# Half a block of a 268 MB copy cut into seven small DMAs over 14, 2, 9, 7, 4, 12 and 16 engines

## The chip, the cores and the metric

The kernel runs on one core of one Trainium2 chip. The metric is the device time of that core in microseconds (us). The kernel does no arithmetic: all of its work is done by the core's 16 DMA engines, which copy from one HBM tensor to another. Two instruction queues issue the DMAs, that of SyncE (SP) and that of ScalarE (ACT).

## The reference

`x` is an 8192 x 8192 float32 matrix (268.44 MB), and the result is `np.fft.ifftshift(x)`. Both sides are even, so each axis is rotated by half its length: the four quadrants of 4096 x 4096 change places diagonally. Row `r` of the output is row `(r + 4096) % 8192` of the input with its left and right halves exchanged.

```python
def setup_inputs():
    return {"x": np.random.randn(8192, 8192).astype(np.float32)}

def reference(x):
    return np.fft.ifftshift(x)
```

## The kernel before

The kernel cuts the output into 64 blocks of 128 rows. One DMA moves one block, from HBM to HBM, with nothing in between: 128 rows of 32 KB, 4 MB in all. Within each row the DMA writes the left half and then the right half, and reads the input's right half and then its left one. The pattern is 128 x 2 x 4096 floats, so it comes apart into 256 contiguous pieces of 16 KB. All 16 DMA engines take part, with 16 pieces each (`rows = ENGINES * 8` gives every engine eight rows). A piece is what the trace calls a packet.

The blocks are dealt to the two queues in groups of eight: of each 1024 output rows, SP's queue takes the first four blocks and ACT's queue the last four. In program order the two queues take turns. SP therefore begins at output row 0 and ACT at row 512, and each issues 32 DMAs:

```python
for first in range(0, R, 8 * rows):
    for row in range(first, first + 4 * rows, rows):
        whole_rows(nc.sync, row)
        whole_rows(nc.scalar, row + 4 * rows)
```

No wait is written by hand. The framework puts a semaphore on every DMA and has eight of them for this kernel: in the trace SP's DMAs use four in turn and ACT's the other four. A queue issues its fifth DMA when its first has landed, its sixth when its second has, and so on. Four blocks of each queue are therefore outstanding until the end. Each of the 16 engines sees two streams of packets, SP's (queue 1 of the profile) and ACT's (queue 10), and serves both of them.

The change touches what the ACT queue issues before its second block (output row 640): the single DMA `whole_rows(nc.scalar, 512)` in the loop's first turn.

Of the kernel before, what the change touches and what calls it, by code (L numbers as in the profile page):

```python
# [1 line left out]

# [4 lines left out]


ENGINES = 16


@with_exitstack
def kernel(
    ctx: ExitStack,
    tc: tile.TileContext,
    x: bass.AP,
    out: bass.AP,
):


    nc = tc.nc
    R, C = x.shape
    hr = R // 2
    hc = C // 2
    rows = ENGINES * 8

    def whole_rows(queue, row):
        src = (row + hr) % R
        queue.dma_start(
            out=bass.AP(out.tensor, out.offset + row * C, [[C, rows], [hc, 2], [1, hc]]),  # L30
            in_=bass.AP(x.tensor, x.offset + src * C + hc, [[C, rows], [-hc, 2], [1, hc]]),
        )

    for first in range(0, R, 8 * rows):
        for row in range(first, first + 4 * rows, rows):
            whole_rows(nc.sync, row)
            whole_rows(nc.scalar, row + 4 * rows)


# [1 line left out]
_INS = ['x']  # L41
_OUTS = [((8192, 8192), 'float32')]


def kernel(**inputs):
    import numpy as _np
    import concourse.bacc as _bacc
    import concourse.tile as _tile
    from concourse import mybir as _mybir
    from concourse.bass_utils import run_bass_kernel_spmd as _run  # L50

    nc = _bacc.Bacc("TRN2", target_bir_lowering=False, num_devices=1)  # L52
    arrays, args = {}, []
    for name in _INS:
        a = _np.ascontiguousarray(inputs[name])
        if a.dtype.kind in "iu":
            a = a.astype(_np.int64)
        arrays[f"in_{name}_dram"] = a
        args.append(nc.dram_tensor(f"in_{name}_dram", a.shape, _mybir.dt.from_np(a.dtype), kind="ExternalInput").ap())
    for i, (shape, dtype) in enumerate(_OUTS):  # L60
        dt = _mybir.dt.from_np(_np.dtype(dtype))
        args.append(nc.dram_tensor(f"out_{i}_dram", shape, dt, kind="ExternalOutput").ap())
    with _tile.TileContext(nc) as tc:
        kernel(tc, *args)
    r = _run(nc, [arrays], core_ids=[0])
    got = tuple(r.results[0][f"out_{i}_dram"] for i in range(len(_OUTS)))
    return got[0]
```

## Time and profile before

| What | Value |
|---|---|
| Time, median of 3 runs | 823.04 us (822.89 to 824.0) |
| The profiled execution's own time | 823.57 us |
| Its span, first to last instruction | 821.8 us |
| DMAs | 32 from SP, 32 from ACT, 4 MB each |
| Moved | 268.44 MB read and as much written |
| A DMA from issue to landing, median | 102.2 us |
| Issue time of one DMA on its queue | 0.6 to 0.9 us for the first four, 0.56 to 0.57 us later |

The compute engines do nothing but clear a few constants (0.2 us), so the only rows to read are those of the DMA engines. The page gives their busy share and the bytes that they moved per second in 40 equal slices of 20.5 us. The trace has every single packet with its start, duration, size and queue. It doesn't name the engine of a packet, but on one engine a packet starts where the last one ended (4 ns before it, in the median), so the 16 sequences can be followed.

### The profile page before, as it was taken

Reading aid. Unit: us, or ns where it says so; the run is one execution under the profiler, and the core shown is the slowest. Engines: PE = TensorE matmul, PEld = TensorE weight load, DVE = VectorE, ACT = ScalarE, POOL = GpSimd, SP = SyncE. Lnnn points to the kernel's source line nnn. Section 1 sums busy time; section 2 is a strip of 40 time slices with the busy share of each in tenths; the row PEclk is TensorE's granted clock in tenths of the full one; section 3 lists DMA queues with packets and bytes.
Section 4 is the critical chain, followed back from the end, with each engine's and each line's share of the span. In section 5 each row is a group of like instructions: output and inputs, shape, how many; then the busy total and the mean of one; then the engine's idle time right before and its main releaser. Section 6 shows DMA issues by size and latency. Waiting matters only on the chain. (4 is left out here: it accounts for less than half of the span.)

```text
span 821.8 us, 109 instructions
## 1 busy us (share of the span) xinstructions
POOL 0.2 (0%) x4
## 2 busy tenths in 40 slices
POOL 0000000000000000000000000000000000000000
DMA  9999999999999999999999999999999999999999
GB/s 302 327 327 322 333 328 320 331 328 327 333 328 332 329 321 331 331 329 330 331 330 329 321 329 329 329 324 332 325 329 329 330 328 329 331 325 331 326 325 296
DMA packets 17408, 268.44 MB, mean 327 GB/s; under 512 B 1024, under 2 KB 1024, under 8 KB 1024
## 3 DMA queue, kind: packets, MB, share of 16 engines
q10 hardware_dynamic: 8704, 134.22, 49.8%
q1 hardware_dynamic: 8704, 134.22, 49.7%
HBM read 268.44 MB, written 268.44 MB: 653 GB/s over the span
## 5 line engine op out<-in xcount | busy, mean ns | idle before, releaser
L52 POOL MEMSET const-bfloat16-1.0<- 128x1 bf16 x1 | 0.1, 102 | 0.0
L52 POOL MEMSET const-uint8-127<- 128x1 uint8 x1 | 0.1, 102 | 0.0
L52 POOL MEMSET const-float32-0.0<- 128x1 f32 x1 | 0.1, 99 | 0.2 <-issue 0.2
L52 POOL MEMSET const-float32-1.0<- 128x1 f32 x1 | 0.1, 99 | 0.0
## 6 DMA issues: line engine op xcount, KB each, us to landing
out_dram<-in_x_dram ACTq DMA_DIRECT2D x32, 4096.0 KB, 102.2
out_dram<-in_x_dram SPq DMA_DIRECT2D x32, 4096.0 KB, 102.2
```

What stands on the lines that cost most here:

```text
L52: nc = _bacc.Bacc("TRN2", target_bir_lowering=False, num_devices=1)
```

## The change

The bytes that are copied, SP's queue and ACT's blocks from row 640 on stay as they are. Of ACT's first block (output rows 512 to 639) the right half of the first 16 rows is taken out and moved by itself, ahead of the loop. It is cut into four strips of 1024 columns (4 KB a row). Each of the first three strips is moved by two DMAs, with 14 and 2 rows, 9 and 7 rows, and 4 and 12 rows; the fourth strip is one DMA of 16 rows. A DMA of `k` rows here is a pattern of `k` x 1024 floats. The rest of the block follows in the loop as two DMAs: the left half of all 128 rows (2 MB), then the right half of the last 112 rows (1.75 MB).

The ACT queue so issues nine DMAs where it issued one.

```diff
+    def half_rows(queue, row, col, dims):
+        src = (row + hr) % R * C + (col + hc) % C
+        queue.dma_start(
+            out=bass.AP(out.tensor, out.offset + row * C + col, dims),
+            in_=bass.AP(x.tensor, x.offset + src, dims),
+        )
...
+    lead = 4 * rows
+    strip = hc // 4
+    for n, k in enumerate((14, 9, 4)):
+        col = hc + n * strip
+        half_rows(nc.scalar, lead, col, [[C, k], [1, strip]])
+        half_rows(nc.scalar, lead + k, col, [[C, ENGINES - k], [1, strip]])
+    half_rows(nc.scalar, lead, hc + 3 * strip, [[C, ENGINES], [1, strip]])
+
     for first in range(0, R, 8 * rows):
         for row in range(first, first + 4 * rows, rows):
             whole_rows(nc.sync, row)
-            whole_rows(nc.scalar, row + 4 * rows)
+            if row + 4 * rows == lead:
+                half_rows(nc.scalar, lead, 0, [[C, rows], [1, hc]])
+                half_rows(nc.scalar, lead + ENGINES, hc, [[C, rows - ENGINES], [1, hc]])
+            else:
+                whole_rows(nc.scalar, row + 4 * rows)
```

## The prediction

> **What bounds the kernel now.** I read the page first: how full the DMA engines are, and how evenly.
>
> ```profile
> span 821.8 us, 109 instructions
> DMA  9999999999999999999999999999999999999999
> GB/s 302 327 327 322 333 328 320 331 328 327 333 328 332 329 321 331 331 329 330 331 330 329 321 329 329 329 324 332 325 329 329 330 328 329 331 325 331 326 325 296
> q10 hardware_dynamic: 8704, 134.22, 49.8%
> q1 hardware_dynamic: 8704, 134.22, 49.7%
> HBM read 268.44 MB, written 268.44 MB: 653 GB/s over the span
> out_dram<-in_x_dram ACTq DMA_DIRECT2D x32, 4096.0 KB, 102.2
> out_dram<-in_x_dram SPq DMA_DIRECT2D x32, 4096.0 KB, 102.2
> ```
>
> The 16 engines are busy for 99.5% of the span, half for each queue, so nothing can be gained by filling gaps. An issue lands 102.2 us later because four blocks of each queue are outstanding, far more than an issue costs. Next I read the waits of SP's queue, to see whether the engines ever wait for an issue.
>
> ```profile
> SPq L29 <- DMA out_dram<-in_x_dram: 696.9, 28, 25.6
> ```
>
> SP waits 28 times for its own earlier DMA, with three more blocks queued behind it: the queue waits for the engines. What counts is then the rate of the engines, so I cut the span into stretches.
>
> ```profile
> 2.00:5.40 3.40, 0.00 (x0) 1.00 0.94 318
> 5.40:13.00 7.60, 0.00 (x0) 1.00 1.04 362
> 13.00:21.00 8.00, 0.00 (x0) 1.00 0.99 311
> 62.00:400.00 338.00, 0.00 (x0) 1.00 1.00 328
> 400.00:764.00 364.00, 0.00 (x0) 1.00 1.00 328
> 764.00:817.00 53.00, 0.00 (x0) 1.00 1.00 327
> 817.80:820.00 2.20, 0.00 (x0) 1.00 0.92 313
> ```
>
> The last column is GB/s, counted by packet starts, so short stretches are rough. From 62 us on it is 328, 328, 327. A packet of 16 KB takes 798 ns in the mean: 1024 packets an engine x 0.7986 = 817.8 us, which with 2.2 us before the first packet and some 1.2 us behind the last is the span. The packets say more:
> - The shortest take 608 to 611 ns (28% of them), the longest over 1100 ns (7%). An engine alone could thus do 16384 / 611 = 26.8 GB/s; at 798 ns it does 20.5, and the rest is lost to something shared.
> - From 2.2 to 5.4 us only SP's packets run; the second to fourth of each engine take 611, 645 to 690 and 611 ns. From 5.4 to 13 us both queues run and the engines are close together: 753 ns with a scatter of 34. Afterwards it is 800 ns with a scatter of 180, to the end.
> - Each engine takes a packet of SP, then one of ACT, in turns of 2 x 0.8 = 1.6 us. The engines stay together in this: at a mean instant 13.0 of 16 are in the same queue (13.3 early, 12.7 late). The 16 parts of one DMA land within 0.4 to 1.1 us, from the first to the last.
>
> **The change part by part.** The seven small DMAs give the engines unlike shares, if a DMA of k rows runs on the first k engines. No row of this trace shows a DMA with k below 16. Adding up the seven: engines 0 and 1 get 7 strips of 4 KB, 2 and 3 get 6, 4 to 6 get 5, 7 and 8 get 4, 9 to 11 get 3, 12 and 13 get 2, 14 and 15 one. In sum 64 strips, 256 KB, the bytes taken from the block. The Trainium skill, in "DMA: Bandwidth & Descriptors" (section on why a DMA increments its semaphore by 16), says that such a DMA takes the largest k up to 16 that divides its slowest dimension, on the lowest-numbered engines; no run here shows it yet.
>
> *Issuing.* ACT issues eight more DMAs ahead of row 640. Its first four issues took 667, 889, 665 and 666 ns, so 8 x 0.67 = 5.4 us, plus waits if the small DMAs use up semaphores: then ACT's left half waits for the first of them, and even SP's second block may wait for one. The cover is SP's first block: 16 packets an engine at 611 ns or more, 9.8 us of work from 2.2 us on. Before, ACT's first packet came at 5.36 us; a small DMA issued up to 5.4 us later has landed by 12 us, and SP's next block follows. Cost 0. If the cover fails, engines idle for some 3 us; if SP runs alone 5 us longer at 640 instead of 753 ns, 0.75 us is gained.
>
> *Smaller pieces.* 64 pieces of 4 KB take the place of 16 of 16 KB, three more per engine. Packets follow each other without a gap, so in proportion they cost nothing (0.15 us each, a quarter of 611); if each cost a whole packet, 3 x 0.61 = 1.8 us. Eight more DMAs write 80 more completion packets of 9 ns, 0.05 us an engine. I take 0.1 us, nearer to the gapless rows.
>
> The Trainium skill speaks against such pieces: "DMA: Bandwidth & Descriptors", Rules for kernel authors, holds that below 64 KB a transfer is mostly overhead. All seven are at most 64 KB; at the page's 2.0 us fixed cost one after the other that would be 14 us, on ACT's queue only, and the sum would stand at about 841 if nothing ran beside them. The trace has SP's packets beside them.
>
> *Unequal shares.* Engine 0 has 12 KB over the mean, engine 15 as much under it. The last engine ends 12/16 of a packet later, 0.46 to 0.6 us; the others leaving earlier help it a little. Cost 0.4 us (0 to 0.6).
>
> *The engines' phases.* While the small pieces pass, one turn is a 16 KB packet of SP and a strip, about 0.8 + 0.2 = 1.0 us. Engine 0 makes seven such turns, engine 15 one, before the regular turns of 1.6 us begin. In a cycle of 1.6 us their starts at 1, 2, ... 7 us fall on 1.0, 0.4, 1.4, 0.8, 0.2, 1.2, 0.6: evenly apart. So instead of 13 of 16 engines about 8 to 10 will be in the same queue at once. Nothing later undoes it: the engines' landings stay within 1.1 us for 820 us, so all progress equally, and an offset given at the start should stay. What that is worth no row shows directly. For a loss: counted over the packets from 14 us on, instants with 14 to 16 engines in one queue move 331.5 GB/s, those with 8 or 9 move 321.4, the mean 327.8; if all instants were like the latter, 2.0% or 16 us. In windows of 12.8 us the slope is 2.5 (+/- 1.5) GB/s per engine, which over four engines is 3%; in windows of 3.2 us it is nothing, -0.2 (+/- 1.0). For a gain: the slices of the page reach from 320 to 333; if all were like the best, 817.8 x (1 - 327/333) = 14.7 us less. Against the gain stands that the most orderly stretch, 5.4 to 13 us, is the fastest with both queues. I take a loss of 0.4%, 3.4 us: near nothing, as the long stretches are flat at 327 to 328 while the order loosens, and on the side that most readings have.
>
> Sum: 823.57 + 0 + 0.1 + 0.4 + 3.4 = 827.5 for the profiled execution, which lay 0.5 us above the median of the runs: 827 us.
>
> **The rivals.**
> *Spreading the phases helps.* Engines that start packets together, whole rows of 32 KB apart, might meet in the same part of the HBM, and not when they are quarters of a packet apart (an estimate of mine; no row shows addresses). For it: the 187 ns between 611 and 798, and the long packets. Against it: the tight start. It decides if the mean packet falls below 796 ns. At the best slice's rate 808 us, at half of it 815 us; I put it at 815. Chance 0.35. The Trainium skill has a row for this ("DMA: Bandwidth & Descriptors", Latency and other measured facts): row pitches at large powers of two slow HBM copies, 207 GB/s at 512 KiB against 214 with 4 KiB of padding. Taken as the gain here, those 3.4% would give 796 us. No run here shows it; the orderly start speaks against it.
> *No effect of the phases*, or the engines fall back into step within some turns, or the k-row DMAs don't spread as I added them up. Then only 0.5 us is left: 823.5 us. For it: 327 to 328 in every long stretch. Chance 0.19.
> *The start stalls.* The semaphores hold up SP's second block behind a small DMA until the first block has run dry, and each of the seven lands alone. Seven times the 3 us between SP's first and ACT's first packet, less 10 us of SP's block, is some 10 us: 833 us. Against it: SP's block covers it, and only one or two of the small ones are in SP's way. Chance 0.05.
> *The forecast*, mixed queues at a small loss: 0.41.
>
> **The numbers.** 0.2% (1.6 us) is about what a measurement of this kernel can tell from no change. Slower: 0.41 + 0.05 = 0.46. Same: 0.19. Faster: 0.35. Cases of both signs hold much of the chance, so the range reaches from near the best slice, 809, to nearly the 2% loss, 838; the forecast's own range is 825 to 838.
>
> **What would show it.** The parts of SP's first block should land about 3 us apart instead of 0.6 (engine 0 has done seven of SP's packets when engine 15 has done under five), ACT's lead block up to 6 us. The engines in one queue at an instant should fall from 13 to 8 to 10, and stay there. The mean packet should be 802 ns in long stretches, 325 to 327 GB/s. In the last us the first and last engine end 1 us apart or more. I am wrong if the order returns to 13 of 16, if long stretches rise above 329, or if the first 20 us show idle engines.

## The result and the profile after

The changed kernel takes 825.29 us (median of 22 runs), the kernel before 823.39 us beside it (22 runs). The ratio is 1.0024 with a 95% interval of 1.0017 to 1.0031: 1.9 us slower. The profiled execution of the changed kernel has a span of 824.3 us, that of before had 821.8.

The page of the changed kernel, cut to the rows that were shown of before:

```profile
span 824.3 us, 117 instructions
DMA  9999999999999999999999999999999999999999
GB/s 300 326 328 322 321 318 330 328 328 329 328 324 329 325 334 329 324 324 329 329 325 330 328 328 325 328 323 324 330 332 328 325 325 330 328 327 324 328 328 301
q1 hardware_dynamic: 8704, 134.22, 49.9%
q10 hardware_dynamic: 8832, 134.22, 49.7%
HBM read 268.44 MB, written 268.44 MB: 651 GB/s over the span
out_dram<-in_x_dram SPq DMA_DIRECT2D x32, 4096.0 KB, 102.5
out_dram<-in_x_dram ACTq DMA_DIRECT2D x31, 4096.0 KB, 102.4
```

The engines are as full as before. Queue 10 (ACT) has 128 more packets: 48 more pieces of data and 80 completions of 4 bytes. (The seven small DMAs move 256 KB, a sixteenth of ACT's first block; the title's "half a block" is too much.) HBM traffic is 651 GB/s where it was 653. By stretches (the last column is GB/s), the changed kernel:

```profile
2.00:20.00 18.00, 0.00 (x0) 1.00 1.00 333
20.00:62.00 42.00, 0.00 (x0) 1.00 1.00 327
62.00:400.00 338.00, 0.00 (x0) 1.00 1.00 327
400.00:764.00 364.00, 0.00 (x0) 1.00 1.00 327
```

The first two stretches of the kernel before:

```profile
2.00:20.00 18.00, 0.00 (x0) 1.00 1.00 335
20.00:62.00 42.00, 0.00 (x0) 1.00 1.00 327
```

The long stretches had 328 before and have 327 now. I added up the bytes of all packets to see when the time is lost:

| Bytes done | Before, us | After, us | Behind, us |
|---|---|---|---|
| 6 MB | 20.32 | 20.41 | 0.1 |
| 30 MB | 93.59 | 94.65 | 1.1 |
| 150 MB | 458.92 | 461.06 | 2.1 |
| 250 MB | 763.61 | 766.79 | 3.2 |
| last packet | 820.58 | 823.21 | 2.6 |

Next to nothing is lost in the first 20 us, where the new DMAs run (0.1 us), and nothing at the end. The loss grows over the whole run, though single rows of the table are uncertain: two executions of the kernel before (this one and e8's below) differ by up to 1.3 us in the same count. The mean 16 KB packet between 62 and 764 us takes 801.6 ns instead of 798.3, which is 0.4% in this pair of executions; the runs say 0.24%.

One thing in the trace I had not drawn: ACT's queue is late. ACT's first issues, before and after (start, time until the last of them is issued):

```profile
0.73 2.97 ACTq L29 DMA_DIRECT2D out_dram<-in_x_dram  x4
0.73 17.36 ACTq L31 DMA_DIRECT2D out_dram<-in_x_dram  x9
```

The last two of the nine are the halves. The left half was issued at 16.9 us, when SP's first block had landed, and at the end ACT runs alone. The two queues in a stretch near the end, before (806 to 818 us: packets, MB, share of the engines' time):

```profile
q10 hardware_dynamic: 127, 2.08, 54.4%
q1 hardware_dynamic: 125, 1.84, 46.4%
```

And in the changed kernel's last stretch (806 to 823 us):

```profile
q10 hardware_dynamic: 362, 5.52, 96.6%
q1 hardware_dynamic: 1, 0.00, 0.0%
```

SP's last packet of data ends 18.5 us before ACT's; before, it was 3.2 us. So after the result there were two explanations for a slightly slower rate: the engines' phases, as predicted, and this late queue.

### The profile page after: what moved, and what is told of

It reads as the page before. It is cut to its first block, busy times and chain, and to the rows that moved or that the text cites. A ratio compares the mean times of both kernels' runs of the same rounds, so it can differ in the third digit from the quotient of the medians.

```text
span 824.3 us, 117 instructions
## 1 busy us (share of the span) xinstructions
POOL 0.2 (0%) x4
```

## The experiments

Each kernel was timed against the kernel before on the same chip (e8 was only profiled). Chips differ: the kernel before takes 811.3 to 811.5 us on some and 823.4 to 823.6 us on others, so only ratios and packets of the same group may be compared.

### e1: seven small DMAs with equal shares

```diff
-    for n, k in enumerate((14, 9, 4)):
-        col = hc + n * strip
-        half_rows(nc.scalar, lead, col, [[C, k], [1, strip]])
-        half_rows(nc.scalar, lead + k, col, [[C, ENGINES - k], [1, strip]])
+    for n in range(6):
+        col = hc + n * strip // 2
+        half_rows(nc.scalar, lead, col, [[C, ENGINES], [1, strip // 2]])
```

> Seven small DMAs stay ahead of the lead block, but each has 16 rows (six strips of 512 columns, one of 1024), so that every engine gets the same 16 KB; ACT's left half still waits for SP's first block. Theory 'phases' (the engines spread over the 1.6 us cycle, and that costs the 0.24%): about 13 of 16 engines in one queue, mean packet 798 to 799 ns, ratio 1.000 to before, 823.4 us. Rival 'late queue' (what costs is that ACT's stream runs some 18 us behind SP's instead of 3, with SP's queue gone for the last 18 us): SP's last packet ends 15 to 18 us before the end, ratio 1.0024, 825.3 us.

Measured: 1.0013 (1.0004 to 1.0021). SP ends 18.6 us ahead, as the rival said. But only 9.7 of 16 engines are in one queue, although every engine got the same bytes. About half of the loss is there without unlike shares, and the loose order too: unlike shares are not needed to loosen it.

### e2: the change without the late start

```diff
-    half_rows(nc.scalar, lead, hc + 3 * strip, [[C, ENGINES], [1, strip]])
...
                 half_rows(nc.scalar, lead, 0, [[C, rows], [1, hc]])
+                half_rows(nc.scalar, lead, hc + 3 * strip, [[C, ENGINES], [1, strip]])
```

> The same seven small DMAs with unlike shares, but the one over 16 rows is issued behind the left half of the block, so that the left half waits only for the first small DMA and not for SP's first block. Theory 'phases': 9 to 10 of 16 engines in one queue, mean packet 802 ns, ratio 1.0024, 825.3 us. Rival 'late queue': SP's last packet ends 3 to 7 us before the end and the ratio falls to 1.000, 823.4 us.

Measured: 1.0005 (0.9996 to 1.0014), with 10.4 engines in one queue. SP ends 11.7 us ahead, more than I had expected. The unlike shares are all there, six of the seven small DMAs still go ahead of the block, and the measured loss is no longer clear of nothing. That spoke for the late queue.

### e3 and e12: only the two halves

```diff
-    strip = hc // 4
-    for n, k in enumerate((14, 9, 4)):
...
-    half_rows(nc.scalar, lead, hc + 3 * strip, [[C, ENGINES], [1, strip]])
...
-                half_rows(nc.scalar, lead + ENGINES, hc, [[C, rows - ENGINES], [1, hc]])
+                half_rows(nc.scalar, lead, hc, [[C, rows], [1, hc]])
```

> No small DMA at all: ACT's first block is only cut into a left and a right half of 128 rows each. Both theories: 13 of 16 engines in one queue, SP about 3 us ahead as before, ratio 1.000 (0.999 to 1.001), 823.4 us. If it is 1.0024 the halves themselves are the cause and both theories fall.

> e3 once more, since it came out at 0.9992 with an interval that just holds 1. A real gain: 0.999 again, SP's last packet behind ACT's. Chance: 1.000.

Measured: 0.9992 (0.9983 to 1.0001), and 0.9997 (0.9988 to 1.0005) the second time. The cut block costs nothing, and the hint of a gain didn't hold. What I had not expected: only 10.2 engines in e3 (11.6 in e12) are in one queue, few as in the slower kernels, at no cost. This alone refutes the measure on which the prediction put its loss.

### e4: the change again

The kernel is the changed one, unaltered.

> The changed kernel unaltered, beside the others on the same chip. Both theories: ratio 1.0024 (1.0015 to 1.0035), mean packet 801 to 803 ns, 9 to 10 of 16 engines in one queue, SP's last packet 18 us before the end.

Measured: 1.0022 (1.0013 to 1.0031), 10.6 engines in one queue, SP 18.8 us ahead, mean packet 789.0 ns on a chip where e3 has 784.9. The loss is there on another chip. Beside it on that chip, the mean of e2's runs is 1.3 us lower (95% interval 0.7 to 1.9), and that of e1's 0.7 us lower (0.1 to 1.3).

### e5 and e6: a late queue without strips or halves

```diff
+    spare = ctx.enter_context(tc.tile_pool(name="spare", bufs=1, space=bass.MemoryType.DRAM))
+    for n in range(8):
+        s = spare.tile([16, 128], mybir.dt.float32, name=f"s{n}")
+        nc.scalar.dma_start(out=s[:], in_=bass.AP(x.tensor, x.offset + n * 128, [[C, 16], [1, 128]]))
+
     for first in range(0, R, 8 * rows):
```

e6 is the same with `nc.sync`. Both copy 64 KB more than the reference asks for, into the spare tensor.

> The kernel before with eight DMAs of 16 x 512 bytes into a spare tensor ahead of ACT's first block, which then waits for the landing of SP's first block. ACT's block is whole, there are no strips and every engine gets the same bytes: only the delay of ACT's queue is left of the change. Theory 'late queue': SP's last packet ends 15 to 19 us before ACT's, ratio 1.0013 to 1.0022, mean packet 0.1 to 0.25% over that of before. Rival 'shapes' (what costs is the strips and the cut first block): ratio 1.000 (0.999 to 1.001). The theory that order within the 1.6 us cycle is what costs asks for fewer engines in one queue where the kernel is slower.

> The mirror image: the eight DMAs go ahead of SP's first block, which waits for ACT's first. 'Late queue' as a matter of the distance alone: 1.0013 to 1.0022 again, with ACT's last packet 15 to 19 us before SP's. If it is the sign of the distance (which stream is ahead in the tensor) that counts: 0.998 to 1.000. 'Shapes': 1.000.

Measured: 1.0013 (1.0004 to 1.0022) with SP 18.6 us ahead, and 1.0015 (1.0006 to 1.0024) with ACT 20.4 us ahead. So about half of the change's loss or more needs neither strips nor halves nor unlike shares, and it doesn't matter which queue is late. Up to here the late queue explained everything.

### e7: one queue alone

```diff
-            whole_rows(nc.scalar, row + 4 * rows)
+            whole_rows(nc.sync, row + 4 * rows)
```

> All 64 blocks on SP's queue, in the same program order; ACT issues nothing. Tests whether it matters at all that the engines serve two streams. The loss that the prediction read from instants with few engines in one queue (321 against 331 GB/s) asks for a gain here, since all 16 are always in one queue: 0.98 to 0.99. If two streams cost nothing: 1.000 (0.998 to 1.002).

Measured: 0.9997 (0.9987 to 1.0006). The page of this kernel:

```profile
GB/s 303 326 330 326 330 328 325 329 330 329 328 330 327 331 329 322 328 334 327 325 330 323 334 328 328 325 324 335 330 327 330 327 330 333 326 330 324 331 329 297
q1 hardware_dynamic: 17408, 268.44, 99.6%
```

With all 16 engines in one queue at all times the rate is that of two queues. Mixing the queues costs nothing, and a late queue can't cost because one runs alone at the end.

### e8: the kernel before, profiled again

> The kernel before, unaltered, for a profile on the same chip as the others. If the order of the engines in the profile before (13 of 16 in one queue) is a property of the kernel, 13 again; if it is a matter of the run or the chip, another number, 10 to 13. Mean packet 785 to 787 ns on a chip that takes 811 us.

Measured: 12.0 engines in one queue, not 13.0, and a mean packet of 797.1 ns (this chip turned out to be one of the 823 us kind, so the expected 785 to 787 ns don't apply). In this execution too, instants with 14 to 16 engines in one queue move 332.9 GB/s and those with 8 or 9 move 323.4. Beside e7 this reads differently from how the prediction read it: the two go together from moment to moment, but keeping all engines in one queue doesn't raise the rate. Over windows of 3.2 us, e8's trace even has the other sign: 1.2 GB/s less for each additional engine in the same queue (standard error 0.6).

### e9: ACT 56 us late

```diff
+            if first > 0:
+                whole_rows(nc.sync, row)
+            elif row == 0:
+                whole_rows(nc.sync, row, 4 * rows)
```

This is e5 with SP's first four blocks as one DMA (`whole_rows` takes the number of rows).

> As e5, but SP's first four blocks are one DMA of 512 rows, so that ACT's first block, waiting for its landing, comes some 50 us late instead of 16. 'Late queue', in proportion to the delay: SP's last packet ends 48 to 52 us before the end, ratio 1.003 to 1.005. 'Late queue' as a matter of being late at all, or of the eight extra DMAs: 1.0010 to 1.0018.

Measured: 1.016 (1.0147 to 1.0173), far outside both. The stretches of the profile show why:

```profile
2.00:20.00 18.00, 0.00 (x0) 1.00 1.00 269
20.00:62.00 42.00, 0.00 (x0) 1.00 0.99 266
62.00:400.00 338.00, 0.00 (x0) 1.00 1.00 333
400.00:764.00 364.00, 0.00 (x0) 1.00 1.00 333
```

While the 512-row DMA runs, the engines are full and yet move only 266 to 269 GB/s: at 20 MB the kernel is 12.7 us behind e12 on the same chip (74.69 against 62.00 us). From there on it is as fast as e12, whose ratio is 1.000:

```profile
2.00:20.00 18.00, 0.00 (x0) 1.00 1.00 342
20.00:62.00 42.00, 0.00 (x0) 1.00 1.00 333
62.00:400.00 338.00, 0.00 (x0) 1.00 1.00 333
400.00:764.00 364.00, 0.00 (x0) 1.00 1.00 333
```

The fence above is e12's. From 20 to 250 MB e9 takes 689.7 us and e12 690.0; the mean packet is 786.2 ns in both. Yet SP ends 55.8 us ahead in e9. So a loss in proportion to the distance of the queues, which is three times that of the change, is excluded. A loss of 0.13% for being late at all would be 0.9 us here, and is less surely excluded: the same stretch takes 700.6, 700.0 and 700.4 us in the single executions of before, e8 and e7. And e9 has e5's eight small DMAs as well: what it shows of the late queue, it shows of them.

### e10: seven tiny DMAs, little delay

The edit is e5's with `range(7)`.

> As e5 with seven DMAs of 16 x 512 bytes instead of eight: ACT's first block then waits only for the first of them. Extra DMAs ahead of the block, but little delay: SP's last packet ends 4 to 9 us before the end. 'Late queue': 1.0002 to 1.0006. If the extra DMAs themselves cost what e5 lost: 1.0013.

Measured: 1.0017 (1.0009 to 1.0025) with SP only 7.0 us ahead. That is what e5 lost, with less than half of e5's distance. So a large distance isn't needed, and e5, e6 and e10 have small DMAs ahead of one queue's first block in common. But e9 has them too, with no lower rate behind its 512-row DMA, so this doesn't show that they are enough.

### e11: unlike shares four times as large

```diff
+    for n, k in enumerate((14, 9, 4)):
+        row, col = lead + n // 2 * ENGINES, n % 2 * hc
+        half_rows(nc.scalar, row, col, [[C, k], [1, hc]])
+        half_rows(nc.scalar, row + k, col, [[C, ENGINES - k], [1, hc]])
+    half_rows(nc.scalar, lead + ENGINES, hc, [[C, ENGINES], [1, hc]])
...
+                half_rows(nc.scalar, lead + 2 * ENGINES, 0, [[C, rows - 2 * ENGINES], [1, hc]])
+                half_rows(nc.scalar, lead + 2 * ENGINES, hc, [[C, rows - 2 * ENGINES], [1, hc]])
```

> The unlike shares of the change four times as large: strips of 16 KB a row, of 32 rows, so that engine 0 has 48 KB over the mean and engine 15 as much under it; the rest of the block is two DMAs of 96 half rows. ACT's rest waits for small DMAs only. The step of the prediction on unequal shares: the last engine ends 48/16 packets later, 1.8 to 2.4 us, so 1.0022 to 1.0029 and first and last engine at least 3.6 us apart at the end. If the other engines' leaving makes up for it: 1.000 to 1.0006, less than 2 us apart.

Measured: 1.0036 (1.0024 to 1.0048), 2.9 us, above both. The last packets of the 16 engines end between 809.9 and 812.1 us, 2.2 us apart, where I had asked for 3.6. The profiled executions of e11 and e12 are 4.2 us apart. From 250 MB to the last packet e11 takes 57.1 us against e12's 55.9, so 1.2 us of that lies in the last stretch. The rest had come before: at 250 MB it is 3.0 us behind e12. Unlike shares do cost at the end, but less than in proportion; at a quarter of this size, as in the change, that is about 0.3 us (an estimate), and the change's own table above shows none.

### All together

Mean packet and order from 62 us on. "Spread" is the time from the first to the last of the 16 parts of a block landing, the median over the blocks of SP and of ACT. "Ahead" is how long SP's last packet of data ends before ACT's. All but the ratio comes from one execution each; those of e5 and e10 were the slowest of their kernels' runs, 1.7 us above the median.

| Kernel | Ratio | Packet, ns | In one queue | Ahead, us | Spread SP, ACT, us |
|---|---|---|---|---|---|
| chips of 823 us: before | 1 | 798.3 | 13.0 | 3.2 | 0.8, 0.7 |
| e8 before again | | 797.1 | 12.0 | 2.9 | 1.3, 1.2 |
| e7 SP only | 0.9997 | 798.0 | 16.0 | | 1.0 |
| e5 ACT late | 1.0013 | 800.0 | 10.8 | 18.6 | 2.7, 1.4 |
| e6 SP late | 1.0015 | 798.7 | 10.2 | -20.4 | 1.5, 2.7 |
| the change | 1.0024 | 801.6 | 9.5 | 18.5 | 2.5, 1.6 |
| chips of 811 us: e3 halves | 0.9992 | 784.9 | 10.2 | -2.5 | 1.2, 1.3 |
| e12 halves again | 0.9997 | 786.2 | 11.6 | -2.4 | 0.9, 1.1 |
| e2 no late start | 1.0005 | 787.1 | 10.4 | 11.7 | 2.2, 3.3 |
| e1 equal shares | 1.0013 | 788.0 | 9.7 | 18.6 | 2.0, 1.5 |
| e10 seven tiny | 1.0017 | 789.2 | 10.5 | 7.0 | 2.2, 2.6 |
| e4 the change | 1.0022 | 789.0 | 10.6 | 18.8 | 2.8, 1.5 |
| e11 shares x4 | 1.0036 | 789.9 | 11.2 | 55.1 | 8.2, 2.1 |
| e9 ACT later | 1.016 | 786.2 | 11.3 | 55.8 | 3.0, 1.4 |

On the 811 us chips the mean packet follows the ratio, but for e9, which loses its time before 62 us: what is lost is lost as a lower rate all along. All six kernels whose ratio is above 1.001, e9 left aside, put seven or eight small DMAs in front of one queue, and in all of them the parts of a block land 2 us apart or more in at least one queue, where the kernels at 1.000 have 0.7 to 1.3 us. The engines work further apart within their blocks. But e9 (3.0 us, with the packet of e12) and e2 (3.3 us, and a ratio that may be 1.000) have that as well. So the spread is a mark of how these kernels begin, and I can't call it the cause.

**What stays open:** why these kernels run 0.1 to 0.2% slower for 800 us. The runs exclude, each as the sole cause, the cut of the block (e3, e12), the mixing of queues (e7, e3), unlike shares (e1, e5, e6, e10), and lateness in proportion to the distance (e9, e10). Seven or eight small DMAs ahead of one queue are common to the slower kernels, but e9 has them and keeps e12's rate, and e2, with six ahead, lies at 1.0005: they are a mark of the slower kernels and not shown as the cause. No run has a late queue without small DMAs ahead of it, so the two can't be parted fully. The 0.7 us between the change and e1 leaves room for a share of unlike shares too.

## Why the prediction was right or wrong

The direction was right: slower, forecast with a chance of 0.46. The size was forecast as 3.9 us over the profiled execution (0.5%) and measured as 1.9 us (0.24%), inside the range. But 3.4 of the 3.9 us came from a step that failed, and without it 0.5 us would have been left, which I counted as no change. The direction was luck in this sense. By its steps:

- **What bounds the kernel:** right. The start costs nothing, the engines stay full, and the time is decided by the rate in the long stretches.
- **Issuing, cost 0:** right in the sum, wrong in how. I let ACT's left half wait for the first small DMA. It waited for SP's first block, since eight semaphores are dealt over both queues and the small DMAs had used up ACT's turns. The cover held: SP's packets filled the engines, 0.1 us is missing at 6 MB. That ACT would be 18.5 us late I didn't see; e9, three times as late, shows no harm in proportion to that.
- **The k-row DMAs run on the first k engines:** right in the number. The trace has 14, 2, 9, 7, 4, 12 and 16 completions for the seven DMAs, one for each engine taken; it names no engine, so it can't show that they are the first ones. The trace agrees in k with the Trainium skill's "DMA: Bandwidth & Descriptors", which has in its section on the semaphore increment of 16 the largest k up to 16 that divides the dimension.
- **Smaller pieces, 0.1 us:** small, as forecast. A 4 KB piece took 191 ns in the mean. Three more pieces are 4 x 191 - 611 = 153 ns an engine beside the shortest 16 KB packet, and nothing beside the 787 ns that a 16 KB packet took in the mean while they ran (5 to 16.5 us). The Trainium skill's rule in "DMA: Bandwidth & Descriptors" (Rules for kernel authors), that transfers under 64 KB are mostly overhead, didn't decide here: 0.1 us is missing at 6 MB, with SP's queue running beside them.
- **Unequal shares, 0.4 us:** not seen at the end. The last packets of the engines ended 0.7 us apart, not 1 us or more; before, it was 0.6. e11 shows the cost where shares are four times as unlike: 1.2 us in the last stretch. Whether they cost something along the way (e4 against e1) stays open.
- **The engines' phases, 3.4 us:** the failed step. What I forecast to see came true: 9.5 engines in one queue instead of 13, to the end, and a mean packet of 802 ns. But the link between the two was wrong. Equal shares loosen the order as much (e1: 9.7), a loose order costs nothing (e3: 10.2 engines at 0.9992), and a perfect one gains nothing (e7). The difference of 331.5 and 321.4 GB/s between instants was a correlation and not a price. I had taken a fifth of it because the long stretches were flat while the order loosened. That flatness, and the windows of 3.2 us without a slope, called for zero. What the runs show in its place is a rate 0.13 to 0.17% lower, so 1.1 to 1.4 us, in e5, e6 and e10, which have small DMAs ahead of one queue and no unlike shares; its cause stays open.
- **Landing spreads as a sign:** the parts of SP's first block landed 1.1 us apart, not 3, and those of ACT's two halves 1.6 us, not up to 6. The strips came one DMA at a time over 5 to 16 us, several of SP's packets between them, and not in close turns as I had drawn it.

Of the rivals, *spreading the phases helps* fell with e1 to e4: their order is as loose, and none is faster than before beyond its interval. (The 214 GB/s that this rival sets against 207 is the rate that the Trainium skill, in "DMA: Bandwidth & Descriptors" (Latency and other measured facts), gives for a padded pitch of 4 MiB, so its 3.4% compares two pitches.) *The start stalls* fell with the first 20 us. *No effect of the phases* was right about the phases and wrong in that only 0.5 us would be left.

## What to carry to other kernels

A correlation between instants of one trace is no price, however clear it looks: look whether it is still there over longer windows and in a second trace, and then build the extreme case (here all packets on one queue), which costs one run. Small DMAs ahead of a saturated stream were hidden at the moment that they ran, and a change that costs nothing there can still be a little slower over all the rest; it took some ten runs beside the kernel before on the same chip to see 0.13%. A test that changes two things at once (e9 is late and has the small DMAs) speaks of both or of neither. Where semaphores are dealt in turn over several queues, a few additional DMAs on one queue can make it wait for another's blocks: count the turns before drawing the start.

## What the runs showed of the hardware that I had not expected

- A DMA of 512 rows instead of 128 (the same 32 KB rows, so 32 rows for each of the 16 engines instead of 8) moves 266 to 269 GB/s instead of 333, with full engines; packets of 5 to 13 us in e9 took 1152 ns instead of 750 in e12. If each engine takes neighbouring rows, the engines are then 1 MB apart instead of 256 KB (no row shows addresses, and no run tests this cause). The Trainium skill's "DMA: Bandwidth & Descriptors" (Latency and other measured facts) has HBM copies slow down at large power-of-two row pitches; the direction agrees.
- One queue moves as much as two: 0.9997 (0.9987 to 1.0006).
- The same kernel takes 811.3 us on one chip and 823.6 on another, 1.5%, six times what this change does.
- 16 engines with shares that differ by 24 KB still end within 0.7 us of each other, though 24 KB take 1.2 us at the mean packet of 801.6 ns; in e11 96 KB, 4.7 us at its 789.9 ns, shrink to 2.2 us. Engines with more to do seem to have been served a little faster.
